# Rotary embedding with ScalarE copies of the exchanged halves, and an index stream at another pace

## The chip, the cores and the metric

One core of one Trainium2 chip runs the whole kernel. The metric is device time in microseconds, the median over several runs of the same program; one execution more was taken with the hardware profiler, and every view of the profile belongs to that one.

## The reference

One decoder layer on 512 tokens of width 1024, all in float32: an input projection into ten parts, a retention group of four heads, an attention group of four heads over keys that an indexer selects, an output projection, a layer norm, a gated feed-forward part of hidden width 2816 and a second layer norm. What the change touches is the rotary embedding of the retention queries and keys, the attention queries and keys, and the indexer's queries and its one key:

```python
def rope(x, positions):
    ...
    x1, x2 = x[..., : d // 2], x[..., d // 2:]
    return jnp.concatenate([x1 * cos - x2 * sin, x1 * sin + x2 * cos], axis=-1)
...
rq = rope(rq.reshape(B, S, RET_HEADS, RET_HEAD_DIM), positions)
rk = rope(rk.reshape(B, S, RET_HEADS, RET_HEAD_DIM), positions)
...
aq = rope(aq.reshape(B, S, ATT_HEADS, ATT_HEAD_DIM), positions)
ak = rope(ak.reshape(B, S, ATT_HEADS, ATT_HEAD_DIM), positions)
iq = rope(iq.reshape(B, S, IDX_HEADS, IDX_DIM), positions)
ik = rope(ik[:, :, None, :], positions)[:, :, 0, :]
sel = indexer_topk(iq, ik, iw, topk)     # relu(q.k), weighted over 8 heads, best 128 keys of each query
```

## The kernel before, in words

Features lie on the 128 partitions and tokens along the free dimension, so a feature tile is 128 x 512, and the two halves of a head that a rotation exchanges are partitions 0 to 63 and 64 to 127.

Products that need full precision are done as three matmuls (`mm3`, L100 to L103): operands are split into a rounded high part and a remainder, and high x high, high x low and low x high are added in one PSUM bank. `split` (L92) makes the parts: ScalarE casts the high part (L93); the remainder is subtracted by VectorE (L98), or ScalarE copies the negated high part (L95) and a DMA from GpSimd's queue adds the source to it (L96). `prepare` does this for a weight three units before its use; the parts go round in four buffers, so a cast also waits until TensorE has finished with the weight of four units before.

The order of the work is written out by hand, and each engine works through its own queue in that order. Main work is a generator that yields after a few matmuls; `run` steps side work at every yield. It goes like this:

- Indexer projection (L224 to L256), five PSUM banks `acc0`, and meanwhile the sine and cosine tables (`rotary_tables`): angles on VectorE, sines on ScalarE, then DMAs that spread them over the partitions (`CT`, `ST` for heads of 128, `CI`, `SI` for the indexer).
- `proj_feature` for eight blocks of 256 features (attention keys, attention queries, retention keys, retention queries), two units of 24 matmuls in each, and in the first block the indexer key (`key`, 24 matmuls more). A finished bank is handed on through `pending`: the first item of the next unit calls `settle`, which runs `put_feature` and with it `rope`. For the first four blocks GpSimd adds the two products (L382) and a DMA puts the sum in place (L383), for the other four GpSimd writes the sum itself (L265).
- `proj_token` for three groups of 512 features with tokens on the partitions; retention runs beside the last two.
- Attention, output projection, norm, feed-forward part, norm.

The side work of the first two stages is the index stream `side`: `index_rope` (four query tiles and the key tile are rotated, split into parts and moved by small DMAs from GpSimd's queue), then `logits` (per query block and indexer head two matmuls into a PSUM bank that is one of four of tag `u`, a ReLU on ScalarE, L454, and a weighted sum on VectorE, L458 and L460), then `topk` (48 rounds of the eight largest and their replacement on VectorE, L471 and L472). Every step of the stream yields a cost, and `pace(side, r)` grants it a credit of `r` at each yield of the main work, so `r` sets how far the stream has come at each point of the main work.

`rope` makes two products, `t1` = tile x cosines and `t2` = exchanged tile x sines. In this version VectorE reads the PSUM bank three times, once for `t1` (L261) and once for each half of `t2` (L262 and L263), where the half that is read lies on the other partitions than the half that is written:

```python
V.tensor_tensor(t1[:, n], src[:, n], ct[:, n], op=ALU.mult)
V.tensor_tensor(t2[0:64, n], src[64:128, n], st[64:128, n], op=ALU.mult)
V.tensor_tensor(t2[64:128, n], src[0:64, n], st[0:64, n], op=ALU.mult)
```

The accumulators of the feature blocks go round in four PSUM banks of tag `d`; small SBUF tiles such as `t1` and `t2` go round in twelve buffers.

Of the kernel before, what the change touches and what calls it, by code (L numbers as in the profile page):

```python
# [12 lines left out]
AF = mybir.ActivationFunctionType  # L13
ALU = mybir.AluOpType
# [39 lines left out]
def hybrid_layer_kernel(ctx: ExitStack, tc: tile.TileContext, xT, x, pos, w0, wf, wt, wo,  # L54
                        wgu, wd, gng, lmg, lmb, lfg, lfb, ident_d, cols_d, masks_d, decay_d, out):
    nc = tc.nc
    V, A, G, T = nc.vector, nc.scalar, nc.gpsimd, nc.tensor
# [9 lines left out]
    def psd(name):  # L67
        return psp.tile([P, 512], F32, tag="d", name=name)
# [4 lines left out]
    def tmp(name, dt=F32):  # L73
        return tp.tile([P, 512], dt, tag="t", name=name)
# [8 lines left out]
    def unit(tag, name, dt=F32):  # L83
        return big.tile([P, 4, S], dt, tag=tag, name=name)

    def dma(dst, src):
        nc.sync.dma_start(dst, src)
# [12 lines left out]
    def mm3(acc, lh, ll, rh, rl, first, last, **kw):  # L100
        T.matmul(acc, lhsT=lh, rhs=rh, start=first, stop=False, **kw)  # L101
        T.matmul(acc, lhsT=lh, rhs=rl, start=False, stop=False, **kw)  # L102
        T.matmul(acc, lhsT=ll, rhs=rh, start=False, stop=last, **kw)  # L103
# [42 lines left out]
    def rotary_tables():  # L146
        both = [tmp("angles"), tmp("turns")]
        (ang, rr), (hh, kk) = ((t[:, :H], t[:, H:]) for t in both)
        trig = [tmp(f"trig{q}").rearrange("p (k c) -> p k c", k=2) for q in range(2)]

        def sub_mul(dst, mult, const_, src):
            V.scalar_tensor_tensor(dst, in0=mult, scalar=-const_, in1=src, op0=ALU.mult, op1=ALU.add)

        def nearest(dst, src, inv):
            V.tensor_scalar(dst, src, inv, MAGIC, op0=ALU.mult, op1=ALU.add)
            V.tensor_scalar(dst, dst, MAGIC, None, op0=ALU.subtract)

        V.tensor_copy(rr, pos_i)
        V.tensor_scalar(ang, rr, cols[:, 0:1], None, op0=ALU.mult)
        nearest(hh, ang, 1.0 / BIG)  # L160
        yield
        for c in BIG_PARTS[:3]:
            sub_mul(ang, hh, c, ang)
        yield
        sub_mul(rr, hh, BIG_TAIL, ang)
        nearest(kk, rr, 1.0 / TWO_PI)
        sub_mul(ang, kk, PI_PARTS[0], ang)
        yield
        sub_mul(ang, hh, BIG_PARTS[3], ang)
        sub_mul(ang, hh, BIG_PARTS[4], ang)  # L170
        sub_mul(ang, kk, PI_PARTS[1], ang)
        yield
        sub_mul(ang, hh, BIG_REST, ang)
        sub_mul(ang, kk, PI_REST, ang)
        nearest(kk, ang, 1.0 / TWO_PI)
        sub_mul(ang, kk, TWO_PI, ang)
        yield
        A.activation(rr, ang, AF.Abs)
        for q in range(2):
            A.activation(trig[q][:, 0], rr, AF.Sin, scale=-1.0, bias=cols[:, 2:3])  # L180
            A.activation(trig[q][:, 1], ang, AF.Sin, scale=(1.0, -1.0)[q])
        queues = (nc.gpsimd, nc.sync, nc.scalar)
        for i in range(2):
            ps, at = slice(64 * i, 64 * i + 64, 2), slice(H * i, H * i + H)
            for q in range(4):
                queues[(4 * i + q) % 3].dma_start(tables[32 * q:32 * q + 32, 2:, at], trig[q // 2][ps])
        for i in range(2):
            ps, at = slice(64 * i, 64 * i + 64), slice(H * i, H * i + H)
            for q in range(2):
                dma(tables[64 * q:64 * q + 64, :2, at], trig[q][ps])  # L190
        yield
# [65 lines left out]
    def rope(dst, src, ct, st, lo=0):  # L257
        t1 = tmp("rt1")
        t2 = tmp("rt2")
        n = slice(lo, S)  # L260
        V.tensor_tensor(t1[:, n], src[:, n], ct[:, n], op=ALU.mult)  # L261
        V.tensor_tensor(t2[0:64, n], src[64:128, n], st[64:128, n], op=ALU.mult)  # L262
        V.tensor_tensor(t2[64:128, n], src[0:64, n], st[0:64, n], op=ALU.mult)  # L263
        if dst is not None:
            G.tensor_tensor(dst, t1[:, n], t2[:, n], op=ALU.add)  # L265
        return t1, t2
# [77 lines left out]
    def weight(ahead=3):  # L344
        k = taken[0]
        taken[0] += 1
        while len(ready) < min(k + 1 + ahead, 2 * limit[0]):
            prepare()
        return ready[k]
# [15 lines left out]
    def settle():  # L365
        while pending:
            pending.pop(0)()

    def dense(items, evac, group=8):
        for n, item in enumerate(items):  # L370
            item()
            if n == 0:
                settle()
            if n % group == group - 1 or n == len(items) - 1:
                yield
        pending.append(evac)

    def put_feature(c, i, acc):
        dst = feats[c // 2][:, 2 * (c % 2) + i]
        if c < 4:  # L380
            t1, t2 = rope(None, acc, CT, ST)
            G.tensor_tensor(t1, t1, t2, op=ALU.add)  # L382
            nc.gpsimd.dma_start(dst, t1)  # L383
        else:
            rope(dst, acc, CT, ST)

    def proj_feature(c):
        for i in range(2):
            h, l = weight(3 if c else 2)
            acc = psd(f"pf{c}_{i}")  # L390

            def items(acc=acc, h=h, l=l):
                for kt in range(KT):
                    cs = slice(kt * P, kt * P + P)
                    yield lambda cs=cs, kt=kt: mm3(acc, h[:, cs], l[:, cs], xh[kt], xl[kt], kt == 0, kt == KT - 1)

            yield from dense(list(items()), lambda i=i, acc=acc: put_feature(c, i, acc), 3)
        if c == 0:
            for kt in range(KT):
                cs = slice(kt * P, kt * P + P)  # L400
                mm3(acc0[0], key[0][:, cs], key[1][:, cs], xh[kt], xl[kt], kt == 0, kt == KT - 1)
                if kt == 0:
                    settle()
                if kt % 3 == 2:
                    yield
            key.append(acc0[0])
# [3 lines left out]
    def proj_token(g):  # L410
        n = KV if g == 1 else S
        accs = [(psu if g == 1 and b > 1 else psd)(f"pt{g}_{b}")[:, :n] for b in range(NB)]

        def evac(b):
            if b == 0:
                tok[g] = unit(("s4", "s5", "s6")[g], ("av", "rv", "grg")[g])
                if n < S:
                    G.tensor_copy(tok[g][:, :, n:], early_v)
            if g == 2:
                sg = tmp("sg")  # L420
                A.activation(sg, accs[b], AF.Silu)
                G.tensor_tensor(tok[g][:, b], sg, gnb, op=ALU.mult)
            else:
                A.copy(tok[g][:, b, :n], accs[b])

        for c in range(4):
            h, l = weight()
            for b in range(NB):
                bs = slice(b * P, b * P + P)
                for k in range(2):  # L430
                    kt = 2 * c + k
                    ks = slice(k * S, k * S + n)
                    mm3(accs[b], xh[kt][:, bs], xl[kt][:, bs], h[:, ks], l[:, ks], kt == 0, kt == KT - 1)
                settle()
                if c == 3:
                    pending.append(lambda b=b: evac(b))
                if b != 1:
                    yield
# [38 lines left out]
    def chain(*its):  # L477
        for it in its:
            yield from it

    def pace(it, r, credit=0.0):
        while True:
            credit += r
            while credit > 0.0:
                c = next(it, 0.0)
                credit -= 1.0 if c is None else c
                if c == 0.0:
                    break
            yield

    def run(main, *sides):
        for _ in main:
            for s in sides:
                next(s, None)
# [158 lines left out]
    def stepwise(f):  # L653
        n = 0
        while True:
            f(n)
            n += 1
            yield
# [59 lines left out]
    lg = chain(*[logits(j) for j in range(1, NB)])  # L718
    tk = chain(*[topk(j) for j in range(1, NB)])
    side = chain(index_rope(), lg, tk)  # L720
    run(chain(*[proj_feature(c) for c in range(4)]), pace(side, 0.85))
    run(chain(*[proj_feature(c) for c in range(4, 8)]), pace(side, 0.85))
    landing = [tmp(f"decay{i}") for i in range(2)]
    for i in range(2):
        dma(landing[i], decay_d[:, i])
    run(proj_token(1), pace(side, 1.7))
    rt["both"] = unit("s7", "both")
    rt["decay"] = rt["both"][:, :2]
    for i in range(2):
# [1 line left out]
    q_lo["k"] = unit("s10", "akl", F32R)  # L731
    splitting = stepwise(split_heads)
    rets = retention()
    run(proj_token(2), pace(side, 1.8), pace(rets, 1.2), splitting)
    mixt[0] = unit("s8", "mrh", F32R), unit("s2", "mrl", F32R)
    tail = chain(rets, att_score(0))
    run(proj_token(0), pace(tail, 1.4), pace(side, 0.55), splitting)
# [862 lines left out]
    for i in range(24):  # L1600
        q, j = WORDER[i]
# [203 lines left out]
```

## Time and profile before

| | |
|---|---|
| median of 3 runs | 605.48 us (604.97 to 606.2) |
| profiled execution | 605.22 us, its span 603.4 us |
| granted TensorE clock, mean | 0.997 |
| TensorE busy | 597.1 us, 99% of the span |
| VectorE busy | 526.0 us, 87% |
| ScalarE busy | 358.9 us, 59% |
| GpSimd busy | 191.7 us, 32% |
| feature projections, first to last matmul | 21.8 to 123.2 us |
| token projections | 123.4 to 203.7 us |

In the lines of the profile PE is TensorE's matmuls, PEld its weight loads, DVE VectorE, ACT ScalarE, POOL GpSimd, SP the queue of most DMAs; a q behind a name is an engine's sequencer, which issues DMAs. L261 is line 261 of the kernel. A line of the timeline gives the start in us, the duration, the engine, the line, the operation, the tiles written and read, their shape and how often, and in brackets the idle time before it and what ended it. A line of a window gives the busy time of each engine, with the number of instructions, then the granted clock, the share of time in which DMA engines were busy, and GB/s. Where a group has three numbers with slashes they are the shortest, the median and the longest duration in ns.

### The profile page before, as it was taken

How to read it: one execution, taken by the hardware profiler on the slowest of the kernel's cores; microseconds unless marked ns; L12 is line 12 of the kernel's file. 1: busy time of each engine (PE TensorE's matmuls, PEld its weight loads, DVE VectorE, ACT ScalarE, POOL GpSimd, SP SyncE). 2: the span in 40 equal slices, each digit the busy share in tenths (PEclk: the TensorE clock that was granted, in tenths of full speed). 3: DMA queues.
4: the chain of work that ended last, by engine and by line, in shares of the span. 5: the costliest groups of instructions: out<-in, count | busy, mean ns of one | idle time of the engine just before them, and what ended most of it. 6: DMA issues, size and time to landing. Idle time of an engine off the chain costs nothing.

```text
span 603.4 us, 9256 instructions
## 1 busy us (share of the span) xinstructions
PE 597.1 (99%) x3229; PEld 518.8 (86%) x3229; DVE 526.0 (87%) x953; ACT 358.9 (59%) x629; POOL 191.7 (32%) x213
## 2 busy tenths in 40 slices
PE   9999999999999999999999999999999999999996
PEld 7988888888888888889998888888888888888885
DVE  6889876898999898989999898989898989799995
ACT  6453444434672676877757677777677756485701
POOL 0038632332463000342003444444443423331110
PEclk9999999999999999999999999999999999999998
DMA  8887864698883776497247888888888998999511
GB/s 298 239 252 196 220 204 122 152 211 246 205 173 105 259 247 209 113 247 148 88 145 195 175 205 172 208 165 205 169 206 179 196 274 223 215 197 264 152 70 70
DMA packets 50766, 114.97 MB, mean 191 GB/s; under 512 B 9072, under 2 KB 23984, under 8 KB 45216
## 3 DMA queue, kind: packets, MB, share of 16 engines
q0 software_dynamic: 25008, 39.00, 37.2%
q1 hardware_dynamic: 25120, 74.59, 36.7%
q10 hardware_dynamic: 592, 0.79, 0.4%
q8 instruction: 25, 0.41, 0.3%
q14 instruction: 21, 0.17, 0.1%
HBM read 77.14 MB, written 2.10 MB: 131 GB/s over the span
## 4 chain that ended last, share of the span: by engine, by line
PE 99%; DVE 1%; issue 0%
PE ga L1014 17%; PE gc L1014 8%; PE pf L101 5%; PE pf L102 5%; PE pf L103 5%; PE gb L1014 4%; PE ga L1027 4%; PE pt L102 4%; PE pt L101 4%; PE pt L103 4%; PE acc L245 3%; PE mx L103 2%; PE mx L101 2%; PE mx L102 2%; PE dl L101 2%; PE dl L103 2%
## 5 line engine op out<-in xcount | busy, mean ns | idle before, releaser
L93 ACT CAST wh<-raw 128x1024 fp32r<-128x1024 f32 x44 | 46.0, 1048 | 30.2 <-issue 11.4
L967 POOL DMA_DIRECT2D t<-t x36 | 30.8, 857 | 79.8 <-DVE t L1067 48.2
L101 PE MATMUL pf<-xh,wh 128*128 128x512 f32 x128 | 50.1, 391 | 0.0
L102 PE MATMUL pf<-xl,wh 128*128 128x512 f32 x128 | 49.9, 390 | 0.0
L103 PE MATMUL pf<-xh,wl 128*128 128x512 f32 x128 | 49.9, 389 | 0.0
L967 POOL DMA_DIRECT2D w<-w x36 | 31.4, 1000 | 41.8 <-DVE w L1053 39.7
L98 DVE TENSOR_TENSOR wl<-raw,wh 128x1024 fp32r<-128x1024 f32 x26 | 32.9, 1273 | 12.2 <-ACT wh L93 12.0
L101 PE MATMUL pt<-wh,xh 128*128 128x512 f32 (+1 forms) x96 | 38.5, 401 | 0.0
L102 PE MATMUL pt<-wl,xh 128*128 128x512 f32 (+1 forms) x96 | 37.0, 386 | 0.0
L103 PE MATMUL pt<-wh,xl 128*128 128x512 f32 (+1 forms) x96 | 36.7, 382 | 0.0
L96 POOL DMA_DIRECT2D wl<-raw x18 | 16.6, 921 | 45.9 <-ACT wl L95 44.8
L509 POOL TENSOR_TENSOR rs<-ve,half 128x1 f32<-128x1 f32 (+1 forms) x10 | 10.3, 1025 | 59.7 <-DVE ve L508 59.5
L103 PEld LDWEIGHTS pf<-xh,wl 128*128 128x128 f32 x128 | 24.0, 188 | 5.2
L101 PEld LDWEIGHTS pf<-xh,wh 128*128 128x128 f32 x128 | 24.0, 188 | 4.6
L102 PEld LDWEIGHTS pf<-xl,wh 128*128 128x128 f32 x128 | 24.0, 188 | 4.5
L471 DVE MAX8 m<-score 128x8 f32<-128x256 f32 (+2 forms) x48 | 26.7, 557 | 1.0
L472 DVE MATCH_REPLACE8 score<-m,score 128x256 f32<-128x256 f32 (+2 forms) x48 | 26.0, 542 | 0.0
L982 POOL DMA_DIRECT2D graw<-graw x17 | 24.7, 1451 | 1.3 <-issue 0.9
L454 ACT ACTIVATE lg<-lg 128x256 f32<-128x256 f32 (+2 forms) x24 | 10.9, 474 | 22.7 <-PE lg L453 20.7
L1116 ACT COPY t<-ga 128x512 f32<-128x512 f32 x17 | 10.0, 587 | 23.8 <-PE ga L1014 23.8
L93 ACT CAST dhp<-sum 128x1024 fp32r<-128x1024 f32 x12 | 12.6, 1054 | 16.3 <-DMA sum<-in_wd_dram 6.9
L103 PEld LDWEIGHTS pt<-wh,xl 128*128 128x128 f32 x96 | 18.0, 188 | 3.3
(1191 smaller groups left out, 2000.0 us busy)
## 6 DMA issues: line engine op xcount, KB each, us to landing
graw<-in_wgu_dram SPq DMA_DIRECT2D x22, 1024.0 KB, 5.1
wl<-raw POOLq DMA_DIRECT2D x18, 512.0 KB, 5.3
raw<-in_wo_dram SPq DMA_DIRECT2D x8, 1024.0 KB, 5.6
raw<-in_wf_dram SPq DMA_DIRECT2D x7, 1024.0 KB, 6.2
raw<-in_wt_dram SPq DMA_DIRECT2D x6, 1024.0 KB, 5.7
r<-in_wd_dram SPq DMA_DIRECT2D x12, 512.0 KB, 6.4
w<-w POOLq DMA_DIRECT2D x36, 128.0 KB, 3.1
t<-t POOLq DMA_DIRECT2D x36, 128.0 KB, 4.7
```

The costliest lines, as they stand in the source:

```text
L93: A.copy(hi, src)
L98: eng_lo.tensor_tensor(lo, src, hi.bitcast(F32), op=ALU.subtract)
L101: T.matmul(acc, lhsT=lh, rhs=rh, start=first, stop=False, **kw)
L102: T.matmul(acc, lhsT=lh, rhs=rl, start=False, stop=False, **kw)
L103: T.matmul(acc, lhsT=ll, rhs=rh, start=False, stop=last, **kw)
L245: T.matmul(acc0[1 + i][:, P:], lhsT=a[:, i * P:i * P + P], rhs=b[kt][:, P:], start=(kt == 0 and p == 0), stop=(kt == KT - 1 and p == 2))
L471: V.max(m8, a)
L472: V.match_replace(out=a, in_to_replace=m8, in_values=a, imm_value=TAKEN)
L967: nc.gpsimd.dma_start(t[:, :Q], t[:, Q:], accum_op=ALU.add)
L982: nc.gpsimd.dma_start(u[:, :S], u[:, S:], accum_op=ALU.add)
L1014: T.matmul(full[:, :Q] if low else full, lhsT=w[:, i * S + k * P:i * S + k * P + P], rhs=rhs, start=first and not low and k == 0, stop=las ...
L1027: T.matmul(gp[n][acc], lhsT=a[:, i * S + k * P:i * S + k * P + P], rhs=parts[q][:, k, b], start=first and j == 0, stop=j == 11, skip_group ...
```

## The change

In `rope` ScalarE copies the two halves of the tile into `t2`, exchanged, and VectorE multiplies the whole of `t2` by the sines in place. The sines stay on the partitions they are written for, not on those of the half that is read, so the sign of the table changes places (`rotary_tables`). Four paces of the index stream change; the last, 0.55, stays.

```diff
-            A.activation(trig[q][:, 1], ang, AF.Sin, scale=(1.0, -1.0)[q])
+            A.activation(trig[q][:, 1], ang, AF.Sin, scale=(-1.0, 1.0)[q])
...
         n = slice(lo, S)
+        A.copy(t2[0:64, n], src[64:128, n])
+        A.copy(t2[64:128, n], src[0:64, n])
         V.tensor_tensor(t1[:, n], src[:, n], ct[:, n], op=ALU.mult)
-        V.tensor_tensor(t2[0:64, n], src[64:128, n], st[64:128, n], op=ALU.mult)
-        V.tensor_tensor(t2[64:128, n], src[0:64, n], st[0:64, n], op=ALU.mult)
+        V.tensor_tensor(t2[:, n], t2[:, n], st[:, n], op=ALU.mult)
...
-    run(chain(*[proj_feature(c) for c in range(4)]), pace(side, 0.85))
-    run(chain(*[proj_feature(c) for c in range(4, 8)]), pace(side, 0.85))
+    run(chain(*[proj_feature(c) for c in range(4)]), pace(side, 1.15))
+    run(chain(*[proj_feature(c) for c in range(4, 8)]), pace(side, 1.15))
...
-    run(proj_token(1), pace(side, 1.7))
+    run(proj_token(1), pace(side, 1.3))
...
-    run(proj_token(2), pace(side, 1.8), pace(rets, 1.2), splitting)
+    run(proj_token(2), pace(side, 1.5), pace(rets, 1.2), splitting)
...
     run(proj_token(0), pace(tail, 1.4), pace(side, 0.55), splitting)
```

## The prediction

> **What bounds the kernel now.** I read the page first (span, busy shares, chain), then TensorE's waits, then busy time in stretches, then VectorE, ScalarE and GpSimd in order of time between 30 and 75 us, where the rotations begin.
>
> ```profile
> span 603.4 us, 9256 instructions
> PE 597.1 (99%) x3229; PEld 518.8 (86%) x3229; DVE 526.0 (87%) x953; ACT 358.9 (59%) x629; POOL 191.7 (32%) x213
> ...
> PE 99%; DVE 1%; issue 0%
> ```
> ```profile
> engine line waited for: us in total, times, longest us
> PE fin L1734 <- ACT diag L1733: 1.3, 1, 1.3
> PE warm L210 <- PEq L1794: 0.8, 1, 0.8
> ```
> TensorE is the chain: it waits twice in the whole execution, once before its first matmul and once in the last strip. A busy engine could still hide slow matmuls, so I look at starts:
> ```profile
> 64.63 0.23 PE pf L101
> 64.86 0.23 PE pf L102
> 65.09 0.24 PE pf L103
> ...
> L101 PE MATMUL pf<-xh,wh x128: 387/389/476, 21.8 to 122.8; 128*128 128x512 f32 x128
> ```
> A 512-column matmul starts every 0.23 us (0.227 over long stretches), so a unit of projection (half a feature block, 24 matmuls) is 5.45 us. The rotations work beside these units:
> ```profile
> core 0: us, PE busy (x) PEld busy (x) DVE busy (x) ACT busy (x) POOL busy (x), PEclk, DMA share, GB/s
> 40.00:60.00 20.00, 20.00 (x90) 16.57 (x89) 19.55 (x28) 9.12 (x14) 15.33 (x21) 1.00 0.75 224
> 60.00:80.00 20.00, 20.00 (x99) 16.77 (x98) 16.29 (x23) 8.79 (x17) 13.05 (x15) 1.00 0.84 208
> 80.00:100.00 20.00, 20.00 (x93) 16.91 (x92) 15.89 (x25) 8.30 (x15) 4.99 (x4) 1.00 0.55 188
> ```
> Between 40 and 60 us VectorE is full (19.55 of 20) and ScalarE less than half; TensorE never waits for either, at full granted clock. So the change relieves an engine that is crowded but does not set the end. It can hardly win; it can lose, where TensorE arrives earlier at something that is not ready.
>
> **The change, part by part.**
>
> *Rotation.* Each of 16 feature and 5 index rotations loses one VectorE multiply and gains two ScalarE copies.
> ```profile
> L261 DVE TENSOR_TENSOR rt<-pf,tables x16: 676/683/693, 39.6 to 123.7; 128x512 f32<-128x512 f32 x16
> L262 DVE TENSOR_TENSOR rt<-pf,tables x16: 692/692/693, 40.2 to 124.4; 64x512 f32<-64x512 f32 x16
> L262 DVE TENSOR_TENSOR rt<-acc,tables x5: 558/558/692, 34.6 to 50.0; 64x384 f32<-64x384 f32 x4, 64x512 f32<-64x512 f32 x1
> 191.32 0.68 DVE L592 TENSOR_TENSOR rzz<-rz,grg 128x512 f32<-128x512 f32 x1
> 202.11 1.52 ACT L424 COPY av<-pt 128x512 f32<-128x512 f32 x3
> ```
> A half of 64 partitions costs as much as a whole tile (0.692 beside 0.683), so one whole multiply replaces two. From two SBUF tiles such an instruction took 0.68: VectorE saves about 0.69 per feature rotation, 0.56 per small index rotation, 16 x 0.69 + 4 x 0.56 + 0.69 = 14 us. ScalarE pays two copies at 1.52/3 = 0.51, if a copy of half the partitions also costs a whole one (nearest row; bounds 0.25 and 0.6): 17 x 1.02 + 4 x 0.85 = 21 us, on an engine with over 10 us free in each 20. In time of TensorE: 0, while these covers hold. Without them a bank of a projection would be freed late; a bank is needed again only three units (16 us) after it is filled.
>
> *What waits anew.* The second multiply waits for ScalarE, whose queue is in order: the copies stand behind the weight casts of the next unit (1.05 each) and the query casts, which themselves wait for VectorE. Behind the waiting multiply stand VectorE's weight remainders and score sums, and GpSimd's add, and behind that GpSimd's weight DMAs.
>
> *The sign* of two sine rows swaps: 0.
>
> *The pace.* The index stream costs 4 x 2.3 + 1.7 + 7.0 + 3.0 = 20.9 up to its first score. At 0.85 a step that is reached at step 25 (20.9/0.85 = 24.6), at 1.15 at step 19 (18.2). Steps 25 and 19 are the same place, two units apart: TensorE reaches the first score 2 x 5.45 = 10.9 us sooner. The whole stream costs 100.4; before, 50 x 0.85 + 12 x (1.7 + 1.8 + 0.55) = 91.1 of it is spent by the end of the last token projection, afterwards 50 x 1.15 + 12 x (1.3 + 1.5 + 0.55) = 97.7. So 6.6 units of top-k leave the attention stage, and the two token stages lighten. TensorE has no wait there to give back: 0, with -0.3 as the limit.
>
> *First deadline: the key halves.*
> ```profile
> 51.45 1.49 DVE L314 TENSOR_TENSOR ks<-rt,rt 128x512 f32<-128x512 f32 x1
> 56.10 2.38 DVE L287 TENSOR_TENSOR kk<-ks,kk 32x512 fp32r<-32x512 f32 x2
> 60.27 0.50 POOL L289 DMA_DIRECT2D kk<-kk  x1
> L452 PE MATMUL lg<-kk,qa x12: 278/333/389, 70.0 to 106.2; 128*128 128x256 f32 x4, 128*128 128x384 f32 x4, 128*128 128x512 f32 x4
> DMA to landing us min/median/max: 1.9/2.3/2.7
> ```
> Before, the halves land at 60.3 + 0.5 + about 2.3 = 63 and are first used at 70.0. Afterwards use is at 70.0 - 10.9 = 59.1. On VectorE they move forward too: one feature rotation (2.1) and one weight remainder (1.2) fall behind them, and seven rotations ahead of them lose a multiply (4 x 0.56 + 3 x 0.69 = 4.3): 56.1 - 7.6 = 48.5 if VectorE never waits. It does: the copies of the key rotation stand on ScalarE behind two weight casts, one remainder, the copy of the index weights and two query casts (3.1 + 0.5 + 0.9), some 2 to 3 us late. So 51 to 52, DMAs out by 55, landed by 57.5: 1.5 us in hand. Cost 0; bounds 0 and 1.
>
> *Second deadline: the banks of the scores.* The four banks of the score tag go round, so the fifth score needs VectorE to have read the first. A score block of 256 columns is two matmuls, 0.24. At the new pace three scores, six projection matmuls and two scores follow each other: the fifth starts at 59.1 + 4 x 0.24 + 6 x 0.227 = 61.4. Before that VectorE must finish the remainder of a weight (1.2) and the rotation of the unit that ended at 21.8 + 6 x 5.45 = 54.5, whose copies are behind these on ScalarE:
> ```profile
> 30.91 1.05 ACT L93 CAST wh<-raw 128x1024 fp32r<-128x1024 f32 x1 [1.76 <-issue]
> 36.34 0.52 ACT L292 CAST qa<-qs 128x384 fp32r<-128x384 f32 x1 [4.38 <-DVE qs L304]
> 52.97 0.62 ACT L284 CAST kk<-ks 128x512 fp32r<-128x512 f32 x1 [1.64 <-DVE ks L314]
> 59.97 1.05 ACT L93 CAST wh<-raw 128x1024 fp32r<-128x1024 f32 x1 [3.53 <-PE pf L102]
> 60.92 1.06 ACT L95 ACTIVATE wl<-raw 128x1024 fp32r<-128x1024 f32 x1
> 64.75 0.41 ACT L325 COPY score<-iwp 128x96 f32<-128x96 f32 x2
> 70.39 0.37 ACT L454 ACTIVATE lg<-lg 128x256 f32<-128x256 f32 x1 [3.51 <-PE lg L453]
> 71.54 0.48 DVE L458 TENSOR_SCALAR score<-lg,iw 128x256 f32<-128x256 f32 x1
> ```
> On time, ScalarE does the index-weight copies (0.6), a cast (1.05) and the two copies (1.0) from 54.5 and is through at 57.2; VectorE ends that rotation by 59, reads the first score at 60.0 to 60.5: 0.9 us in hand. But from 30.9 on ScalarE has 23 us of work to do by then (nine casts and remainders of weights 9, eight query casts 3.3, eight small copies 3.4, twelve large ones 6.1, the key cast and the index weights 1.7). Two waits for VectorE stay, at the first query cast and at the key cast: 4.38 and 1.64 now, I estimate 2.5 each then. 30.9 + 23 + 5 = 58.9 instead of 57.2 eats the margin. Then GpSimd:
> ```profile
> 66.91 2.59 DVE L98 TENSOR_TENSOR wl<-raw,wh 128x1024 fp32r<-128x1024 f32 x1 [0.91 <-ACT wh L93]
> 80.30 1.22 DVE L98 TENSOR_TENSOR wl<-raw,wh 128x1024 fp32r<-128x1024 f32 x1 [0.47 <-ACT wh L93]
> 66.75 1.66 POOL L382 TENSOR_TENSOR rt<-rt,rt 128x512 f32<-128x512 f32 x1
> ```
> The remainder that began under GpSimd's add took 2.59 instead of 1.22 and ended 1.1 after the add: it stood still while GpSimd worked. The old sine multiplies, which read PSUM, all took 692 to 693 though adds ran beside some of them; the new one reads two SBUF tiles, like the remainder, so I count it as exposed. The Trainium skill (GPSIMD Engine Reference, Key points) says the same: GpSimd shares its SBUF interfaces with VectorE and contends with VectorE instructions that have two SBUF inputs; these rows agree. One such collision on this stretch costs up to 1.37. So the stall at the fifth score lies between 0 and 1.7 + 1.37 - 0.9 = 2.2. I take 0.5, nearer the lower end, because the bursts are short and TensorE, once it has waited, gives VectorE time for the next banks; a second wait at the ninth score is bounded by one read, 0 to 0.8, taken at 0.
>
> *Sum.* 0 (rotation) + 0 (key) + 0.5 (banks) + 0 (later stages) = +0.5 us. The profiled execution took 605.22 us (span 603.4 and 1.8 around it), the runs 604.97 to 606.2, median 605.48. 605.22 + 0.5 = 605.7, and against the median 606.0. I give 606.0.
>
> **The rivals.**
>
> *Slower, by the banks.* The wait at the fifth score is real and repeats at the ninth: 1.2 to 3 us, 607.5. For it: the margin above vanishes with either a late ScalarE or one collision; VectorE at 19.55 of 20. Against: it has 14 us less to do. It decides when VectorE's first read of a score (L458) ends after about 62.6. One form of it: copies and first multiply read the same PSUM bank; if they go one after another, VectorE's part of each rotation starts up to 1.0 us later and the score reads behind it too, 607.0. No row of before shows two engines at one bank, so I give this form 0.13 of the rival's 0.33. The Trainium skill (PSUM — Partial Sum Buffer, Terms) says that two engines must not be at one bank and quadrant at once, reads included.
>
> *Slower, by the weights.* The new multiply, stopped by GpSimd, delays GpSimd's add, and the DMA that completes a weight's low half stands behind it in that queue, for instance for the seventh unit at 54.5:
> ```profile
> 49.42 0.94 POOL L96 DMA_DIRECT2D wl<-raw  x1
> wl<-raw POOLq DMA_DIRECT2D x18, 512.0 KB, 5.3
> ```
> Issued at 49.4 and landing by the median 5.3 later, it comes in at 54.7, so there is nothing in hand there; each collision ahead of it would add up to 1.4: 607 to 610, say 608.5. Against: the index rotations ahead of it are shorter now.
>
> *Faster.* VectorE's relief shortens something after all. TensorE's only late wait is 1.3 us in the last strip, which the change does not touch; the limit is 604.2.
>
> *The change does not relieve VectorE,* since its multiply waits for the copies as long as the removed one took: then the stretch from 40 to 60 us stays full, and as TensorE has three units in hand the time is 605.5 to 606. It counts with the forecast.
>
> **How the numbers follow.** About 0.2% (1.2 us) is what a measurement of this kernel can tell from no change. Forecast with the last rival 0.53; slower by the banks 0.33; slower by the weights 0.09; faster 0.05. The forecast alone spans 604.9 to 606.7. The range reaches from the lowest run less a little, 604.8, to both bank waits at their upper ends and a little of the weights, 605.48 + 2.2 + 0.8 + 0.3 = 608.8.
>
> **What would show it.** VectorE's rotation groups: two lines instead of three, 0.68 each, and 14 us less; ScalarE some 21 us more. The first score near 59 instead of 70, the last about 20 us sooner. Right, if TensorE still has its two waits only and no score matmul is listed as waiting for VectorE or a DMA. Wrong, if TensorE waits at a score (banks: for VectorE; key halves: for a DMA) or at a projection matmul for a low half; or if the multiply is often far above 0.68, which is the collision.

## The result, and the profile after

The changed kernel takes 610.3 us (median of 4 runs, 609.41 to 611.5) against 605.23 us for the kernel before beside it: a ratio of 1.0082, interval 1.0061 to 1.0104. It is slower by 5 us, by more than the range of the prediction allowed. The profiled execution took 610.07 us, 4.9 more than the one of before, and so did its span. Numbers of lines are one higher behind the rotation: L453 and L454 are the score matmuls, L459 and L461 VectorE's reads of the scores, L455 the ReLU; L261 and L262 are now ScalarE's copies, L263 and L264 VectorE's multiplies.

The head of the page, and TensorE's waits:

```profile
span 608.3 us, 9304 instructions
PE 598.3 (98%) x3229; PEld 519.0 (85%) x3229; DVE 511.3 (84%) x932; ACT 382.0 (63%) x671; POOL 191.5 (31%) x213
```
```profile
engine line waited for: us in total, times, longest us
PE lg L453 <- DMA kk<-kk: 1.9, 1, 1.9
PE fin L1735 <- ACT diag L1734: 1.3, 1, 1.3
PE lg L453 <- DVE score L459: 1.1, 1, 1.1
PE warm L210 <- PEq L1795: 0.8, 1, 0.8
PE lg L453 <- DVE score L461: 0.6, 1, 0.6
```

VectorE gave up 14.7 us and ScalarE took on 23.1, as intended. Three waits are new, all at score matmuls: one for the key halves and two for banks that VectorE has not read yet. Where they lie, in the timeline of TensorE:

```profile
58.97 0.39 PE L103 MATMUL pf<-xh,wl 128*128 128x512 f32 x1
61.31 0.36 PE L453 MATMUL lg<-kk,qa 128*128 128x256 f32 x1 [1.95 <-DMA kk<-kk]
...
63.60 0.28 PE L454 MATMUL lg<-kk,qb 128*128 128x256 f32 x1
65.02 0.39 PE L453 MATMUL lg<-kk,qa 128*128 128x256 f32 x1 [1.14 <-DVE score L459]
```

The first score should have started at 58.97 + 0.23 = 59.2 and started 2.1 us later; the fifth came 1.3 us late (63.60 + 0.12, against 65.02), the ninth about 0.8. That is 4.2 us, and the feature stage as a whole shows it:

```profile
L103 PE MATMUL pf<-xh,wl x128: 387/389/398, 22.4 to 127.8; 128*128 128x512 f32 x128
```

The same row in the kernel before:

```profile
L103 PE MATMUL pf<-xh,wl x128: 387/389/397, 22.3 to 123.2; 128*128 128x512 f32 x128
```

A product takes three matmuls, and this row is the third of them. From its first to its last start the stage lasts 127.8 - 22.4 = 105.4 us; before it was 123.2 - 22.3 = 100.9. The 4.5 us are nearly the whole loss. I use this length below as a second measure beside the time of a run, since it leaves out the rest of the kernel.

What VectorE and ScalarE did up to the first read of a score (timelines of VectorE, ScalarE and GpSimd):

```profile
59.26 0.69 DVE L263 TENSOR_TENSOR rt<-pf,tables 128x512 f32<-128x512 f32 x1 [1.53 <-ACT rt L262]
59.87 0.68 DVE L264 TENSOR_TENSOR rt<-rt,tables 128x512 f32<-128x512 f32 x1
60.72 2.65 DVE L98 TENSOR_TENSOR wl<-raw,wh 128x1024 fp32r<-128x1024 f32 x1 [0.17 <-ACT wh L93]
63.30 0.68 DVE L263 TENSOR_TENSOR rt<-pf,tables 128x512 f32<-128x512 f32 x1
63.90 0.68 DVE L264 TENSOR_TENSOR rt<-rt,tables 128x512 f32<-128x512 f32 x1
64.50 0.47 DVE L459 TENSOR_SCALAR score<-lg,iw 128x256 f32<-128x256 f32 x1
```
```profile
53.23 0.62 ACT L285 CAST kk<-ks 128x512 fp32r<-128x512 f32 x1 [2.63 <-DVE ks L315]
```
```profile
59.62 1.07 ACT L93 CAST wh<-raw 128x1024 fp32r<-128x1024 f32 x1
60.71 0.58 ACT L261 COPY rt<-pf 64x512 f32<-64x512 f32 x1
61.31 0.58 ACT L262 COPY rt<-pf 64x512 f32<-64x512 f32 x1
```
```profile
60.70 1.58 POOL L383 TENSOR_TENSOR rt<-rt,rt 128x512 f32<-128x512 f32 x1
```

The unit that ended near 55 is copied by ScalarE only at 60.71 to 61.89, behind a weight cast. ScalarE has worked without a gap since 53.23; before that it stood 2.63 us at the key cast, waiting for the key rotation on VectorE, which itself had stood 1.51 us for ScalarE's copies. VectorE's remainder began together with GpSimd's add and ended 1.1 us after it (2.65 us where 1.22 is usual), and the read of the first score ended at 64.97, 5.8 us after TensorE could have started that score. The key is as late: four DMAs leave GpSimd between 54.85 and 56.84, in the midst of a weight load of 1 MB. The groups of the key halves and the issues of that stretch:

```profile
DMA to landing us min/median/max: 4.9/5.3/5.8
```
```profile
raw<-in_wf_dram SPq DMA_DIRECT2D x1, 1024.0 KB, 5.6
kk<-kk POOLq DMA_DIRECT2D x4, 64.0 KB, 5.3
```

Before, the four left at 58.8 to 60.3, when that load (issued at 54.2, 5.1 us to landing) was at its end, and landed in 2.3. Throughout the later stages (attention, feed-forward) TensorE's waits are those of before.

### The profile page after: what moved, and what is told of

Its sections match the earlier page's. It is cut to its first block, busy times and chain, and to the rows that moved or that the text cites. A ratio compares the mean times of both kernels' runs of the same rounds, so it can differ in the third digit from the quotient of the medians.

```text
span 608.3 us, 9304 instructions
## 1 busy us (share of the span) xinstructions
PE 598.3 (98%) x3229; PEld 519.0 (85%) x3229; DVE 511.3 (84%) x932; ACT 382.0 (63%) x671; POOL 191.5 (31%) x213
## 4 chain that ended last, share of the span: by engine, by line
PE 87%; DVE 4%; DMA 3%; ACT 3%; issue 1%; SPq 0%; ACTq 0%; DVEq 0%
PE ga L1015 17%; PE gc L1015 8%; PE gb L1015 4%; PE ga L1028 4%; PE pt L102 4%; PE pt L101 4%; PE pt L103 3%; PE pf L102 3%; PE pf L103 3%; PE pf L101 3%; PE mx L103 2%; PE mx L101 2%; PE mx L102 2%; PE dl L102 2%; PE dl L101 2%; PE dl L103 2%
## 5 line engine op out<-in xcount | busy, mean ns | idle before, releaser
L968 POOL DMA_DIRECT2D t<-t x36 | 30.9, 857 | 79.7 <-DVE t L1068 48.1
L263 DVE TENSOR_TENSOR rt<-pf,tables 128x512 f32<-128x512 f32 x16 | 11.0, 688 | 12.6 <-ACT rt L262 9.9
```

The lines of the kernel that those rows point to most:

```text
L968: nc.gpsimd.dma_start(t[:, :Q], t[:, Q:], accum_op=ALU.add)
```

## The experiments

All times are medians beside runs of the kernel before on the same chip (605.2 to 605.6 us); the ratio is to those runs. The last column is the length of the feature stage in the profiled execution, read as above.

| kernel | us | ratio, interval | feature stage, us |
|---|---|---|---|
| before | 605.23 | | 100.9 |
| changed | 610.3 | 1.0082, 1.0061 to 1.0104 | 105.4 |
| new rotation, old paces | 607.01 | 1.0023, 1.0011 to 1.0036 | 101.9 |
| old rotation, new paces | 613.85 | 1.0135, 1.0111 to 1.0159 | 109.3 |
| changed, scores three steps later | 606.74 | 1.0021, 1.0005 to 1.0037 | 101.7 |
| changed, first multiply ahead of the copies | 621.5 | 1.0264, 1.0233 to 1.0295 | 115.2 |
| changed, key moved by copies | 610.48 | 1.0082, 1.0068 to 1.0095 | 104.9 |
| changed, weight load behind the key | 610.43 | 1.0092, 1.0072 to 1.0112 | 105.4 |
| changed, adds on VectorE | 609.94 | 1.0071, 1.0059 to 1.0083 | 105.2 |
| changed, copies ahead of the cast | 608.71 | 1.0051, 1.0037 to 1.0065 | 102.6 |
| new rotation, old paces, copies ahead | 605.92 | 1.0012, 1.0003 to 1.0021 | 100.9 |
| changed, copies ahead, one step later | 606.99 | 1.0043, 1.0020 to 1.0065 | 101.4 |
| changed, copies ahead, two steps later | 606.21 | 1.0010, 1.0000 to 1.0019 | 100.9 |

### Which half of the change costs

Theory: the scores, 11 us earlier, meet key halves and banks that are not ready. Rival: the new rotation makes everything late.

The new rotation alone keeps the four paces of before:

```diff
-    ... pace(side, 1.15)) ... pace(side, 1.3)) ... pace(side, 1.5), ...
+    ... pace(side, 0.85)) ... pace(side, 1.7)) ... pace(side, 1.8), ...
```

> The new rotation with the old paces (0.85, 0.85, 1.7, 1.8). Theory M (meeting): the 5 us are waits of TensorE at three score matmuls (2.1, 1.3 and 0.8 us in the profile after), which arise because the scores come 11 us sooner; at the old pace the first score is back near 70 us, the key halves land by 62, and the time is that of before, 605.2, within 0.8 us. Theory R (rotation): ScalarE's copies and the order of the two engines at one PSUM bank (VectorE stood 12.3 us for the copies in the profile after) make everything late whatever the pace: 608 to 610.

The new paces alone take the kernel before and edit the same four numbers the other way.

> The old rotation with the new paces (1.15, 1.15, 1.3, 1.5). Theory M: VectorE has the longer rotations to do ahead of the same early scores, so the key halves are at least as late and the banks later: 608 to 611, with waits at the first and fifth score. Theory R: the pace by itself costs nothing, since without the copies VectorE does not stand still: 605 to 606. A third outcome, 606.5 to 608, would say that both parts are needed for the whole of it.

The third kernel is the changed one, with its first score three steps later:

```diff
         halves_k(ks)
-        yield 7.0
+        yield 10.45
```

> The changed kernel, but the step after the key halves costs 10.45 instead of 7.0, so the first score comes three steps (5.4 us) later and all that follows it too; nothing else changes. Theory M: the first wait (key halves landing about 61.3 against a need at 59.1) has 3 us in hand and is gone, the waits for banks are gone or under 0.5 us: 605.2 to 606. Theory R: the work on VectorE and ScalarE is the same and the time stays at 608 or more.

Measured: 607.01, 613.85 and 606.74. The paces cost 8.6 us with the old rotation and 3.3 with the new one; the rotation costs 1.8 at the old paces and *saves* 3.6 at the new ones. So the early scores are the larger part, and the rival is wrong as it was put. But the first theory missed all three numbers: the rotation does cost something by itself, so that even with the scores three steps later 606.74 us lie above its 605.2 to 606 (a wait of 0.5 us for a bank is left there, and the feature stage is 0.8 us longer than before), and the paces alone are worse than the whole change. The reason for the latter is in the waits of the kernel with the old rotation and the new paces, and in its granted clock (windows: length, then busy time of TensorE, its weight loads, VectorE, ScalarE, GpSimd, then the clock):

```profile
PE lg L452 <- DMA kk<-kk: 4.3, 1, 4.3
```
```profile
65.20:69.60 4.40, 4.40 (x15) 3.74 (x15) 1.59 (x4) 1.60 (x5) 0.90 (x2) 0.50 0.61 199
```

The key halves land 7.2 us (median) after their issue, TensorE stands 4.3 us, and then it computes at half clock for more than 4 us. With two small waits (0.5 and 0.2 us) this explains most of the 8.4 us by which its feature stage is longer: 5.0 us of waiting, and 2.2 us lost at half clock in this window alone. The waits for banks are nearly gone here, since VectorE had 4.3 us to catch up. Why the key DMAs took 7.2 us here and 5.3 in the changed kernel, no run shows.

### What VectorE waits for in the new rotation

In the new rotation at the old paces one bank of the scores is 0.8 us late. The timelines of VectorE and ScalarE there:

```profile
72.06 0.48 DVE L461 SCALAR_TENSOR_TENSOR score<-lg,iw,score 128x256 f32<-128x256 f32 x1 [1.14 <-ACT lg L455]
75.62 0.69 DVE L263 TENSOR_TENSOR rt<-pf,tables 128x512 f32<-128x512 f32 x1 [3.08 <-ACT rt L262]
76.23 0.68 DVE L264 TENSOR_TENSOR rt<-rt,tables 128x512 f32<-128x512 f32 x1
76.83 1.07 DVE L461 SCALAR_TENSOR_TENSOR score<-lg,iw,score 128x256 f32<-128x256 f32 x2
```
```profile
72.33 1.05 ACT L93 CAST wh<-raw 128x1024 fp32r<-128x1024 f32 x1
73.28 1.05 ACT L95 ACTIVATE wl<-raw 128x1024 fp32r<-128x1024 f32 x1
74.36 0.58 ACT L261 COPY rt<-pf 64x512 f32<-64x512 f32 x1
74.96 0.58 ACT L262 COPY rt<-pf 64x512 f32<-64x512 f32 x1
```

VectorE stands 3.1 us, with a score ready behind it, until ScalarE has cast a weight, negated it and copied the two halves. The kernel before went straight on with the first multiply of that rotation (its timeline of VectorE):

```profile
72.81 0.68 DVE L261 TENSOR_TENSOR rt<-pf,tables 128x512 f32<-128x512 f32 x1
```

Two experiments turn this order round, one at each end. The first lets VectorE read the bank first, so that the copies wait for VectorE:

```diff
-        A.copy(t2[0:64, n], src[64:128, n])
-        A.copy(t2[64:128, n], src[0:64, n])
         V.tensor_tensor(t1[:, n], src[:, n], ct[:, n], op=ALU.mult)
+        A.copy(t2[0:64, n], src[64:128, n])
+        A.copy(t2[64:128, n], src[0:64, n])
```

> The changed kernel with the first multiply written ahead of the two copies, so at a rotation's bank VectorE goes first and ScalarE waits for it. If VectorE's wait for the copies (12.3 us in sum, 1.5 us at the key rotation) is what makes the key halves late, they go out 1.5 us sooner, before the 1 MB weight load that starts at 55 us, land in 2.3 instead of 5.3, the first wait vanishes: 606 to 608. If ScalarE, now standing behind VectorE, is what everything else waits for, the time is 610 or more.

Measured: 621.5 us, the second of the two answers. ScalarE now stands behind VectorE's backlog with the casts of the next weight in its queue, and TensorE waits for those too. The clock adds to it: it was 0.50 from 55 to 60 us, after the wait for the cast.

```profile
PE lg L453 <- DVE score L459: 3.6, 1, 3.6
PE pf L101 <- ACT wh L93: 3.3, 1, 3.3
```

The other experiment leaves copies and multiply as changed and issues the rotation of a finished unit ahead of the next weight's preparation:

```diff
+            settle()
             h, l = weight(3 if c else 2)
```

> The changed kernel, but the rotation of a finished unit is issued ahead of the preparation of the next weight, so ScalarE's two copies no longer stand behind a cast of 1.05 us (or a cast and a negated copy, 2.1 us). Theory that ScalarE's queue makes VectorE late: VectorE's rotations and with them the score reads come 1 to 2 us earlier; the waits at the fifth and ninth score (2.1 together) go, the wait for the key stays near 2: 607.8 to 609 us. Rival that the order on ScalarE does not matter, or that the weights become late instead: 610 us or more.

> The new rotation at the old paces, with the copies issued ahead of the preparation of the next weight. In the kernel with the new rotation at the old paces a score bank came 0.8 us late because VectorE stood 3.1 us at the head of a rotation for two copies that were queued behind a cast and a negated copy. Theory: that wait goes and the time is that of the kernel before, 605.0 to 606.2 us. Rival (the new rotation costs its 1.8 us in another way, for instance later in the token projections): 606.8 to 607.5 us.

Measured: 608.71 and 605.92 us, both inside the first theory's numbers. The former's profiled execution, 607.35 us, is the fastest of six; the two with the lowest granted clock, 0.995 against 0.998 to 1.000, took 609.5 and 610.4. Its waits, and VectorE and GpSimd ahead of the first read of a score:

```profile
PE lg L454 <- DMA kk<-kk: 1.4, 1, 1.4
PE fin L1736 <- ACT diag L1735: 1.3, 1, 1.3
PE warm L210 <- PEq L1796: 0.8, 1, 0.8
```
```profile
61.46 1.22 DVE L98 TENSOR_TENSOR wl<-raw,wh 128x1024 fp32r<-128x1024 f32 x1
62.60 0.48 DVE L460 TENSOR_SCALAR score<-lg,iw 128x256 f32<-128x256 f32 x1
```
```profile
61.80 2.03 POOL L383 TENSOR_TENSOR rt<-rt,rt 128x512 f32<-128x512 f32 x1
```

The two waits for banks are gone, because the first score is read 1.9 us earlier; the wait for the key is left. Two things make up the 1.9 us, and the experiment does not part them. ScalarE's copies end at 60.17 instead of 61.89. And the line moves VectorE's part of the rotation too: the remainder of the weight now stands behind it, begins ahead of GpSimd's add and takes 1.22 us instead of 2.65. With a collision of that size there, the first read would have come only some 0.5 us earlier (an estimate, 1.9 - 1.43). At the old paces, where the key is in time, the feature stage is back at its 100.9 us; by the ratios 0.7 us are left of the 1.4 that the rotation costs there, by the medians 0.4 of 1.8. TensorE shows 0.3 of it at the first retention matmul, a wait for VectorE that is there without the extra line too; the rest I cannot place.

### One bill or three

The three waits add up to 4.2 us, but they are met one after another, and the first also gives VectorE time for the second. Does taking one away help? The key was moved without DMAs:

```diff
-                nc.gpsimd.dma_start(kl[1][d].bitcast(F32), kl[0][s].bitcast(F32))
-                nc.gpsimd.dma_start(kh[d].bitcast(F32), kh[s].bitcast(F32))
+                G.tensor_copy(kh[d], kh[s].bitcast(F32))
...
+                G.tensor_copy(kl[1][d], kl[0][s].bitcast(F32))
```

> The changed kernel, but the four small pieces of the key halves are moved by copies on GpSimd instead of by DMAs, so nothing of the key waits for the DMA engines. Theory 'one bill in three waits': the first read of a score on VectorE (64.5 us) stands behind work that does not depend on the keys, so the fifth score still cannot start before 65.0; the wait for the key goes and the wait for the fifth score grows from 1.3 to about 3.4 us: 609.5 to 610.8 us. Rival 'three bills': the waits are independent and the 2.1 us of the key simply go: 607.8 to 608.6 us.

And the DMAs were kept, but the weight load held back behind them:

```diff
             raws.append(raw_tile(f"raw{len(raws)}"))
+            if keys_sent:
+                keys_sent.pop()
+                nc.gpsimd.memset(raws[-1][:, 0], 0.0)
             dma(raws[-1], stream[len(raws) - 1][0])
```

> The changed kernel, with a memset of half of the raw buffer on GpSimd behind the four DMAs of the key halves, so that the weight load of 1 MB which started at 55 us starts at about 58. Theory that the key DMAs landed late because they met this load: their landing falls from 5.3 to 2.2 to 3 us and TensorE no longer waits for a DMA; as the first read of a score still ends near 65 us, the wait for the fifth score grows instead and the time stays at 609.5 to 610.6 us. Rival (the small DMAs are slow for another reason, for instance the addition of a low half that runs beside them): landing stays at 5 us and the wait for the key at 2. A time of 607.5 to 608.5 us with the key wait gone would contradict that the waits stand for one bill.

Measured: 610.48 and 610.43 us, no gain from either. The second is the clean one. The groups of the key halves and the waits:

```profile
DMA to landing us min/median/max: 1.8/1.9/2.0
```
```profile
PE lg L459 <- DVE score L465: 3.3, 1, 3.3
...
PE lg L459 <- DVE score L467: 0.6, 1, 0.6
```

Without the weight load beside them the DMAs land in 1.9 instead of 5.3 us, so the load was the cause. (VectorE subtracts a remainder beside the four issues in both kernels, from 54.67 and from 55.30 us, so that is not it.) TensorE no longer waits for a DMA; it waits 3.3 us at the fifth score instead of 1.9 and 1.1, and the feature stage is 105.4 us as before the edit. The first read of a score ends 42.6 us after the start of the stage in both, so holding back the load delayed nothing else on that path. I rest the comparison on the stage, at full clock around these waits in both profiles: the profiled execution, 614.33 us, has one more wait of 2.2 us in the attention stage, and the other five runs, 610.2 to 611.7 us, show a granted clock of 0.995 to 0.996, so some of their time may be clock. In the kernel that copies the key, the number is right by luck: there the remainder did not meet GpSimd's add, the fifth score waited only 2.1, but TensorE then ran at half clock for 3 us and gave most of the difference back:

```profile
PE lg L455 <- DVE score L461: 2.1, 1, 2.1
```
```profile
64.60:67.60 3.00, 3.00 (x9) 2.32 (x7) 0.97 (x2) 2.95 (x5) 1.55 (x3) 0.50 0.58 141
```

The share of the collision was tried with VectorE doing GpSimd's adds of the first eight feature rotations (`V.tensor_tensor(t1, t1, t2, op=ALU.add)` in place of `G.tensor_tensor`).

> The changed kernel, but VectorE, not GpSimd, adds the two products of the first eight feature rotations: 8 x 0.68 us more for VectorE, and the collisions with GpSimd at 40.6, 46.2 and 60.7 us (0.9, 1.0 and 1.4 us) go. Theory that the collision at 60.7 makes the first read of a score late: the fifth score waits 0.5 to 1 us less, the key still 2 us: 609.3 to 610.0 us. Rival that VectorE's load is what counts: the waits at the scores grow by 0.5 to 2 us: 610.8 to 612.5 us.

Measured: 609.94 us, within the theory's numbers but not told apart from the changed kernel's 610.3. The remainder took 1.22 there and the first read ended at 63.74, 1.2 us earlier; the fifth score waited 0.5 instead of 1.3, but at the ninth the added work came back, 1.5 instead of 0.8. The collision is real, and taking it away by more work on VectorE gains nothing that shows.

### A version without the waits

With the copies ahead of the cast only the wait for the key is left, which a later start should fill with projection matmuls: `yield 8.15` (one step, 1.8 us) or `yield 9.3` (two steps) behind `halves_k`.

> The changed kernel with the copies issued ahead of the next weight, and the first score one step of the index stream (1.8 us) later, all other paces as changed. Theory: the one wait left in that kernel (1.4 us for the key) is filled with projection matmuls, TensorE keeps only the two waits of before: 605.2 to 606.2 us. Rival (moving the scores moves the wait along, to the fifth score or a later bank): 606.5 to 608 us.

> As the kernel before it, but two steps (3.6 us) later. Theory: no wait is left, 605.0 to 606.0 us, within 0.3 us of the kernel with one step. Rival: scores that come later fall on the next weight's cast on ScalarE and a bank is late again, 606 to 607 us. Faster than the kernel before by more than 0.2% is not expected by either, since TensorE had no wait there that these edits touch.

Measured: 606.99 us with one step, a miss by the median: its eight runs lie between 605.9 and 611.23, while its profiled execution took 606.1 and waits 0.2 us for the key. Margins are tenths of a microsecond there, but why the runs scatter, no trace shows. With two steps it takes 606.21 us; the upper end of the theory was 606.0. TensorE's waits in the latter are those of the kernel before and no others:

```profile
PE fin L1736 <- ACT diag L1735: 1.3, 1, 1.3
PE warm L210 <- PEq L1796: 0.8, 1, 0.8
```

It is level with the kernel before (1.0000 to 1.0019) and no faster. None of these versions beats it, as none touches a place where it waited.

## Why the prediction was wrong

- *TensorE bounds the kernel and the change can hardly win*: right. VectorE's 14 us bought nothing in any version. The rotation saves time (3.6 us) only at the new paces, and there most of it is not VectorE's work: with the old rotation the first key DMA left 0.4 us later, but the four took 7.2 us to land against 5.3, and half clock followed the long wait.
- *Rotation*: VectorE's saving is right (14 forecast, 14.7 measured). ScalarE's copies start 0.60 apart for 512 columns, the upper bound and not the 0.51 taken: 23.1 us more instead of 21. That it costs TensorE nothing was wrong by 1.8 us even at the old paces, where the sum has no other term. The text under *What waits anew* had named the path, the copies behind the weight casts and the score sums behind the waiting multiply, and the price was worked out for the new paces alone.
- *First score near 59*: right for when TensorE was ready (59.2). The last came some 15 us sooner, not 20.
- *First deadline*, cost 0 with bounds 0 and 1: wrong, 2.1 us. The margin was 57.5 against 59.1; the pieces were in place at 61.3. Of the 3.8 us between, 1.3 are the last issue (56.3 instead of 55), since VectorE's subtraction ends at 55.3 and the four DMAs leave GpSimd 0.5 us apart, and some 2.5 are the landing: 2.3 was taken from a stretch just behind a weight load, and the move put the DMAs into it.
- *Second deadline*, 0.5 with bounds 0 and 2.2: this is the step that sets the result. With the key in time it costs 3.3 at the fifth score and 0.6 at the ninth. The parts had been named, ScalarE late and one collision of 1.37, but ScalarE's lateness was mis-sized: it was to be through at 58.9 and was at 61.9. From 30.9 to 61.9 it was busy for 24.75 us, not 23 (the listed parts add up to 23.5), and idle for 6.2, not 5. Most of the first is the copies, 10.8 us of busy time where 3.4 + 6.1 = 9.5 were taken, since they start 0.48 and 0.60 us apart and not 0.43 and 0.51. The second is mostly a third wait for VectorE, 1.15 us at another query cast, beside 1.86 and 2.63 at the two that were forecast. The row of windows:

```profile
30.90:61.90 31.00, 29.05 (x133) 23.84 (x132) 24.68 (x30) 24.75 (x43) 20.09 (x26) 1.00 0.74 226
```

  The collision came on top, at its full size (2.65 instead of 1.22). And the upper end was given up in favour of 0.5 because bursts are short, which no row supported.
- *The rivals*: the banks' rival, 0.33, was the right one, with 607.5 too small a size. Its form, copies and multiply one after another at a PSUM bank, is what the trace shows: in the list of VectorE's waits between 20 and 250 us the first multiply waits for the second copy 8 times, and it never starts before that copy's end. The multiply needs nothing from the copies; with the multiply written first, the copies wait for it instead (2.69 us at the first rotation), so the order is that of the program. The Trainium skill (PSUM — Partial Sum Buffer, Terms) says two engines must not be at one bank and quadrant at once, reads included; this order agrees with it.

```profile
DVE rt L263 <- ACT rt L262: 12.3, 8, 2.6
```

- *The sum*: key and banks were costed as two deadlines to be added. They share one path: what TensorE waits at the first is not waited at the second. Adding them is right only for the part by which the second is later than the first. With the key at 0 this did not move the forecast.

## What to carry to other kernels

When work moves to an engine with free time, ask what stands ahead of it in that engine's queue at that moment, not how much time is free: two copies of 0.6 us behind a cast and a negated copy held VectorE for 3.1 us, where the multiply that they replaced took 0.69. One line that issued the rotation ahead of the cast removed both waits for banks, in part because it also moved VectorE's remainder out from under GpSimd's add. When a consumer is pulled forward, price its inputs in the stretch where they will now run, with the transfers that are there. And when several waits follow each other on one engine, take the later deadline, not the sum, and expect that removing the first only moves the time to the next.

## What the runs showed of the hardware

TensorE's clock halved after some of these waits and not after others: to 0.50 for over 4 us after a wait of 4.3, to 0.50 for 3 us after one of 2.1 us, but not at all after one of 3.3 (the windows behind it, in the kernel with the load held back):

```profile
64.30:70.00 5.70, 5.34 (x26) 4.25 (x26) 2.88 (x7) 4.34 (x8) 2.54 (x3) 1.00 0.74 214
```

The Trainium skill (TensorE: Matmul & The Clock Gate, Part 1) says that the clock halves after an idle window of about 3.4 us and that the window runs freely. A free-running window fits the irregularity; a length of 3.4 does not fit the halving after 2.1 us. What decides stays open. At half the clock, 4.4 us lose 2.2 and 3 us lose 1.5: a wait of a few microseconds can cost that much beyond its own length.

Of VectorE's subtraction of two SBUF tiles and GpSimd's add, the one that began later was stretched. In the changed kernel, and again with the weight load held back, the add began 0.02 us ahead, and the subtraction took 2.65 us instead of 1.22. With the copies ahead of the cast the subtraction began 0.34 us ahead and took its 1.22, and the add took 2.03 us where others take 1.28. So an order that lets VectorE begin first can move the cost to GpSimd, which here had time for it.
